# Some 3,900 multiplications of constants ahead of a decoder step's first product

## The chip, the cores and the metric

The kernel runs on one core of one Trainium2 chip. The metric is the device time of one execution in microseconds (us). Before the change it is 1596.22 us, the median of two runs (1596.18 and 1596.26).

## The reference

One inference step of a one-layer decoder for 256 prompt tokens and 8 samples of 4 tokens each, 288 tokens in all, width 2048. Conditioning vectors (one for the prompt, one for each sample, 9 in all) give six modulation vectors; the tokens go through a normalised, modulated projection, a short gated convolution beside a spatial gating mixer, an output product, and a gated feed-forward layer.

```python
mod = (silu(c) @ w_ada + b_ada)                    # 9 x 12288, the conditioning product
h   = rms(x, g_mix) * (1 + sc_m) + sh_m
proj = h @ w_in                                    # 2048 x 9216
b_gate, c_gate, hc, u, v, ga, gb = split(proj)
ya = b_gate * conv(c_gate * hc)                    # width 3
yb = gelu(u) * (causal w_sg @ rms(gelu(v), g_v) + b_sg)
merged = sigmoid(ga) * (ya @ w_pa) + sigmoid(gb) * (yb @ w_pb)
x = x + gt_m * (merged @ w_out)
gate, up = split((rms(x, g_ffn) * (1 + sc_f) + sh_f) @ w_ffn_in)
x = x + gt_f * ((silu(gate) * up) @ w_ffn_out)     # d_ff 5632
y = rms(x, g_final)
```

Beside y, the last rows of the convolution's input and the normalised v rows are returned. All inputs and outputs are fp32.

## The kernel before, in words

All of it is held with features on the partitions and the 288 tokens along the free dimension. A weight tile of 128x128 is the stationary operand, an activation tile of 128x288 the moving one.

**The products.** Weights and activations are split into a high part in fp32r and a low part, the fp32r of what is left. `triple` (L239 to L244) then issues three matmuls: high by high, high by low, low by high. The casts for the high parts run on ScalarE (L471), the subtractions for the low parts on VectorE (L478, L258). These three lines of `triple` are most of the program. Tiles of the moving operand, made by `slot`, begin 7 elements (28 bytes) into a buffer of 320 (`LEADIN`, `PITCH`). In the first stretch they are 298 columns wide, elsewhere 288. For fp32 and fp32r there is no separate weight load in the program; the profile still shows one LDWEIGHTS record for each matmul record.

**The conditioning product** (`Ada.run`, L403) is plain fp32: the 9 vectors, padded to 32 columns, are stationary, and up to 512 columns of `w_ada` move. Four such matmuls with the same accumulator tile `ada` go to four groups of 32 columns of the array (`tile_position=(0, 32 * j)`). A plain fp32 matmul is two records in the profile, so four make eight.

**The beginning.** `warm` (L595) multiplies a bf16 tile of ones by itself, 288 columns wide, into a PSUM tile `idle` that nobody reads. TensorE's program begins with `warm(24)`, the first conditioning block `a0[0]`, `warm(5)`, `a0[1]` with `warm(6)` in its middle, 2 and 6 more of `warm`, and then the first projection stream `w0` with 298 columns. After eight tiles of `w0` comes `a1[0]`, after eleven `a1[1]`.

**What sets the order.** TensorE's order is the order in which the code is written (a manual schedule). VectorE, ScalarE and SyncE are ordered by a scheduler until the head of the program starts, and by hand in the head. All weights are loaded by SyncE's queue (SP) into one pool of 7 buffers of 8 KB per partition, tag `raw`; a load waits until the earlier tile of its buffer has been read for the last time, and all later loads wait behind it on the queue. The head loads both blocks of `a0` (`raw`, 1 MB each), four pieces of `w0` with the first tile of `x` between them, both blocks of `a1`, the second tile of `x`, then `wK`, `wA` and the rest of `x`.

**PSUM.** Tiles tagged `main` turn through four banks; `idle` holds the first.

Of the kernel before, what the change touches and what calls it, by code (L numbers as in the profile page):

```python
# [8 lines left out]
F32 = mybir.dt.float32  # L9
F32R = mybir.dt.float32r  # L10
# [4 lines left out]
P = 128  # L15
D = 2048
T = 288
# [10 lines left out]
RAW = 7  # L28
# [60 lines left out]
def decoder_kernel(tc, d):  # L89
    nc = tc.nc  # L90
    from contextlib import ExitStack

    with ExitStack() as es:
        def pool(name, bufs=1, **kw):
            return es.enter_context(tc.tile_pool(name=name, bufs=bufs, **kw))

        pc = pool("const")
        pw = pool("wstream")
        pslot = pool("slots", MAIN)
        pkept = pool("kept", KEPT)  # L100
        ptmp = pool("tmp", 5)
        pps = pool("psum", 4, space=bass.MemoryType.PSUM)
        with tc.manual_schedule(engines={nc.tensor.engine}):
            _body(tc, nc, d, pc, pw, pslot, pkept, ptmp, pps)


def _body(tc, nc, d, pc, pw, pslot, pkept, ptmp, pps):
    ids = [0]

    def nm(s):  # L110
        ids[0] += 1
        return f"{s}_{ids[0]}"

    def const(name, shape, dt=F32):
        return pc.tile(shape, dt, tag=name, name=name)
# [12 lines left out]
    def psmain():  # L128
        return pps.tile([P, 512], F32, tag="main", name=nm("pm"), bufs=4)
# [4 lines left out]
    V, A, G, PE, SY = nc.vector, nc.scalar, nc.gpsimd, nc.tensor, nc.sync  # L134
# [232 lines left out]
    class Step:  # L367
        defer = False
        raw = None
# [218 lines left out]
    wb = const("wb", [P, 288], BF16)  # L588
    G.memset(wb, 1.0)
    idle = psmain()  # L590
# [498 lines left out]
        tail.close()  # L1089


    rh1 = h1.__getitem__
    def at(main, plan):
        out, n = [], 0
        for s in main:
            out.append(s)
            if isinstance(s, Blk):
                n += 1
                out += plan.pop(n, [])
        assert not plan  # L1100
        return out
# [71 lines left out]
    n = len(steps)  # L1173
# [30 lines left out]
    for s in steps:  # L1204
# [11 lines left out]
        i = pos[id(s)]  # L1216
# [124 lines left out]
```

## Time and profile before

| | |
|---|---|
| median of two runs | 1596.22 us |
| profiled execution | 1596.24 us |
| its span, first to last instruction | 1594.5 us |
| outside the span | 1.74 us |
| TensorE matmul records | 12641 |
| VectorE, ScalarE busy | 1015.9 us, 735.7 us |
| first conditioning matmul starts at | 7.00 us |
| first projection matmul starts at | 12.09 us |

A matmul record's length is modelled and overlaps the next: what one matmul costs is the distance between starts, which the timeline gives to 10 ns, or the count in a stretch that is all matmuls. In the timeline, a row is the start in us, the time covered in us, the engine, the line, the operation, the tiles, stationary shape, moving shape, and how many records the row joins.

### The profile page before, as it was taken

Reading aid. Unit: us, or ns where it says so; the run is one execution under the profiler, and the core shown is the slowest. Engines: PE = TensorE matmul, PEld = TensorE weight load, DVE = VectorE, ACT = ScalarE, POOL = GpSimd, SP = SyncE. Lnnn points to the kernel's source line nnn. Section 1 sums busy time; section 2 is a strip of 40 time slices with the busy share of each in tenths; the row PEclk is TensorE's granted clock in tenths of the full one; section 3 lists DMA queues with packets and bytes.
Section 4 is the critical chain, followed back from the end, with each engine's and each line's share of the span. In section 5 each row is a group of like instructions: output and inputs, shape, how many; then the busy total and the mean of one; then the engine's idle time right before and its main releaser. Section 6 shows DMA issues by size and latency. Waiting matters only on the chain.

```text
span 1594.5 us, 31602 instructions
## 1 busy us (share of the span) xinstructions
PE 1583.4 (99%) x12641; PEld 1518.7 (95%) x12641; DVE 1015.9 (64%) x2200; ACT 735.7 (46%) x1366; POOL 20.9 (1%) x65
## 2 busy tenths in 40 slices
PE   9999999999999999999999999999999999999997
PEld 8998999898998998999898999999999999999997
DVE  6676788877755667667844555555655555555565
ACT  5633344643444434456633444444444444444464
POOL 0000000000000000011000000000000000000000
PEclk9999999999999999999999999999999999999999
DMA  9887866777778766654577556443464534645341
GB/s 382 331 323 285 322 240 218 282 271 313 283 293 333 277 258 228 254 175 170 176 309 268 217 183 217 164 168 118 165 233 163 169 126 164 228 162 174 113 164 60
DMA packets 59476, 357.88 MB, mean 224 GB/s; under 512 B 6720, under 2 KB 10176, under 8 KB 28608
## 3 DMA queue, kind: packets, MB, share of 16 engines
q1 hardware_dynamic: 59040, 355.73, 60.6%
q8 instruction: 99, 1.62, 0.4%
q14 instruction: 49, 0.40, 0.1%
q10 hardware_dynamic: 288, 0.13, 0.0%
HBM read 352.74 MB, written 3.09 MB: 223 GB/s over the span
## 4 chain that ended last, share of the span: by engine, by line
PE 97%; DVE 2%; issue 0%; ACT 0%; DVEq 0%; POOL 0%; ACTq 0%; POOLq 0%
PE pm L239 30%; PE pm L244 30%; PE pm L242 30%; PE ada L403 5%; DVE lo L478 1%; PE pm L595 1%; DVE s L337 0%; DVE st L1070 0%; DVE s L318 0%; DVE t L331 0%; PE px L902 0%; ACT hi L471 0%; PE px L901 0%; PE px L213 0%; PE px L848 0%
## 5 line engine op out<-in xcount | busy, mean ns | idle before, releaser
L239 PE MATMUL pm<-s,hi 128*128 128x288 f32 (+1 forms) x3750 | 1095.4, 292 | 0.3 <-DVE s L998 0.3
L242 PE MATMUL pm<-s,hi 128*128 128x288 f32 (+1 forms) x3750 | 1090.6, 291 | 0.1
L244 PE MATMUL pm<-s,lo 128*128 128x288 f32 (+1 forms) x3738 | 1088.1, 291 | 0.0
L471 ACT CAST hi<-raw 128x512 fp32r<-128x512 f32 (+1 forms) x963 | 585.5, 610 | 774.2 <-PE pm L242 738.2
L478 DVE TENSOR_TENSOR lo<-raw,hi 128x512 fp32r<-128x512 f32 (+1 forms) x849 | 578.6, 683 | 420.0 <-ACT hi L471 407.6
L239 PEld LDWEIGHTS pm<-s,hi 128*128 128x128 f32 x3750 | 702.1, 187 | 15.7 <-issue 13.3
L242 PEld LDWEIGHTS pm<-s,hi 128*128 128x128 f32 x3750 | 702.2, 187 | 0.3 <-DVE s L337 0.3
L244 PEld LDWEIGHTS pm<-s,lo 128*128 128x128 f32 x3738 | 699.9, 187 | 0.0
L258 DVE TENSOR_TENSOR lo<-raw,hi 128x512 fp32r<-128x512 f32 x111 | 74.6, 676 | 28.0 <-ACT hi L471 27.2
L403 PE MATMUL ada<-raw,cs 128*32 128x512 f32 (+2 forms) x1152 | 88.0, 452 | 0.0
L403 PEld LDWEIGHTS ada<-raw,cs 128*32 128x32 f32 x1152 | 30.9, 110 | 44.5 <-issue 41.6
L793 DVE TENSOR_TENSOR s<-pm,s 128x288 f32<-128x288 f32 x72 | 32.8, 456 | 18.5 <-PE pm L244 18.2
L311 ACT CAST s<-t 128x288 fp32r<-128x288 f32 (+1 forms) x76 | 32.9, 433 | 19.1 <-DVE t L825 12.5
L313 DVE TENSOR_TENSOR s<-t,s 128x288 fp32r<-128x288 f32 (+1 forms) x76 | 35.0, 461 | 6.5 <-ACT s L311 5.7
L353 DVE SCALAR_TENSOR_TENSOR x<-pm,mod,x 128x256 f32<-128x256 f32 x79 | 37.5, 475 | 0.0
L991 DVE SCALAR_TENSOR_TENSOR t<-t,pm 128x288 f32<-128x288 f32 x42 | 19.1, 454 | 19.3 <-PE pm L244 19.3
L785 DVE TENSOR_TENSOR s<-pm,s 128x288 f32<-128x288 f32 x48 | 21.8, 454 | 9.9 <-PE pm L244 9.2
L352 DVE TENSOR_TENSOR t<-pm,mod 128x32 f32<-128x32 f32 x79 | 15.1, 192 | 16.5 <-PE pm L244 15.9
L776 DVE TENSOR_TENSOR s<-s,rb 128x288 f32<-128x288 f32 x48 | 21.5, 448 | 0.0
L181 ACT ACTIVATE t<-x 128x288 f32<-128x288 f32 x29 | 12.9, 444 | 17.4 <-DVE x L356 17.4
L186 DVE TENSOR_TENSOR acc<-acc,t 128x288 f32<-128x288 f32 x33 | 15.0, 455 | 8.2 <-ACT t L181 8.2
L770 DVE SCALAR_TENSOR_TENSOR s<-pm,s 128x256 f32<-128x256 f32 x36 | 17.3, 481 | 2.7 <-PE pm L244 2.7
(168 smaller groups left out, 479.5 us busy)
## 6 DMA issues: line engine op xcount, KB each, us to landing
raw<-in_fi SPq DMA_DIRECT2D x84, 1024.0 KB, 4.8
raw<-in_a SPq DMA_DIRECT2D x64, 1024.0 KB, 7.5
raw<-in_f SPq DMA_DIRECT2D x64, 704.0 KB, 4.0
raw<-in_wD SPq DMA_DIRECT2D x34, 1024.0 KB, 5.3
raw<-in_aE SPq DMA_DIRECT2D x16, 1024.0 KB, 9.8
raw<-in_wo SPq DMA_DIRECT2D x16, 1024.0 KB, 5.8
raw<-in_wC SPq DMA_DIRECT2D x19, 768.0 KB, 4.4
raw<-in_pa SPq DMA_DIRECT2D x8, 1024.0 KB, 6.0
```

The lines of the kernel that those rows point to most:

```text
L239: PE.matmul(out, wh, ah, start=first, stop=False)
L242: end_ = PE.matmul(out, wh, al, start=False, stop=turn and last)
L244: end_ = PE.matmul(out, wl, ah, start=False, stop=last)
L258: lows.pop(0)[1]()
L311: A.copy(hi, a)
L313: V.tensor_tensor(lo, a, hi.bitcast(F32), ALU.subtract)
L353: V.scalar_tensor_tensor(x[:, m, :TP], ps[:, :TP], mod[:, gt0 + m, 0:1], x[:, m, :TP], ALU.mult, ALU.add)
L403: PE.matmul(acc[32 * j : 32 * j + 32, :w], cs[:, kt, :], self.raw[:, o : o + w], start=kt == 0, stop=kt == 15, tile_position=(0, 32 * j), ...
L471: A.copy(hi, self.raw[:, s * 128 : e * 128])
L478: sub()
L785: return V.tensor_tensor(part[m], ps[:, :T], part[m], ALU.add)
L793: V.tensor_tensor(a, ps[:, :T], a, ALU.add)
```

## The change

A function `bench` is added and called once, before the first conditioning block is built. It takes four tiles of the `raw` pool: `f`, which VectorE fills with 0.75, and three fp32r copies of it, `r0` by VectorE, `r1` and `r2` by ScalarE. It takes three more banks of the `main` PSUM tiles beside `idle`. Then TensorE multiplies these constants, with `start` and `stop` set on each matmul. Nothing reads the products; nothing that the kernel returns is changed.

```diff
+    def bench():
+        f = pw.tile([P, 2048], F32, tag="raw", name=nm("bench"), bufs=RAW)
+        V.memset(f, 0.75)
+        rs = []
+        for i in range(3):
+            r = pw.tile([P, 2048], F32R, tag="raw", name=nm("benchr"), bufs=RAW)
+            A.copy(r, f) if i else V.tensor_copy(r, f)
+            rs.append(r)
+        r0, r1, r2 = rs
+        outs = [idle] + [psmain() for _ in range(3)]
+        def st(r, i, o=0, m=P):
+            q = o + P * (i % 3)
+            return r[:, q : q + m]
+        def mm(i, s, m, n=512):
+            PE.matmul(outs[i % 4][:, :n], s, m, start=True, stop=True)
+        def group(i, j, s, m, n, w=32):
+            PE.matmul(outs[i % 4][w * j : w * j + w, :n], s, m,
...
+                tile_position=(0, w * j), ...)
+        for i in range(48):
+            PE.matmul(idle[:, :T], wb[:, :P], wb, start=True, stop=True)
+        for n in (512, 510, 508, 496, 480, 448, 384, 320):
+            for o in range(0, 64, 8):
+                for q in range(3):
+                    for i in range(6):
+                        mm(0, st(r0, i), r2[:, o + 512 * q : o + 512 * q + n], n)
+        for o in range(64):
+            for i in range(12):
+                mm(i // 3, st(r0, i), r2[:, o + 512 * (i % 3) : o + 512 * (i % 3) + 512])
+        for o in (0, 7, 16, 23):
+            for b in range(0, 64, 4):
+                for i in range(4):
+                    mm(i, st(r0, i, b), r2[:, o : o + 512])
+                    mm(i, st(r0, i, b), r2[:, o + 512 : o + 1024])
+                    mm(i, st(r1, i, b), r2[:, o : o + 512])
+        for n in (512, 256, 128):
+            for o in (0, 7):
+                for one in (0, 1):
+                    for i in range(8):
+                        for j in range(4):
+                            m = o + 384 * j
+                            group(0 if one else j, j, f[:, 32 * i : 32 * i + 32], f[:, m : m + n], n)
+        for n in (128, 256):
+            for i in range(8):
+                for j in range(4):
+                    m = 7 + 384 * j
+                    group(0, j, f[:, 32 * i : 32 * i + 32], f[:, m : m + n], n)
+                for q in range(6):
+                    mm(1, st(r0, q), r2[:, 7 : 519])
+        for n in (512, 288):
+            for o in (0, 7):
+                for i in range(12):
+                    group(0, 0, st(r0, i, 0, 32), r2[:, o : o + n], n)
...
+        for n in (32, 64):
+            for i in range(48):
+                PE.matmul(idle[:, :n], st(r0, i), r2[:, 7 : 7 + n], start=True, stop=True)
+            for i in range(48):
+                PE.matmul(idle[:, :n], st(r0, 0), r2[:, 7 : 7 + n], start=True, stop=True)
+        for i in range(24):
+            PE.matmul(idle[:, :32], f[:, P * (i % 8) : P * (i % 8) + P], f[:, 7:39], start=True, stop=True)
+        for i in range(24):
+            PE.matmul(idle[:, :P], f[:, P * (i % 8) : P * (i % 8) + P], f[:, 7 : 7 + P], start=True, stop=True)
+
+    bench()
```

The two loops left out are 120 and 96 more 512-wide fp32r matmuls (`mm`, L1110) on `r0`, `r1` and `r2` with moving tiles from columns 7, 519 and 1031.

TensorE's program at its start, before: `wb` is the bf16 tile, `pm_100` is `idle`, `raw_103` the first block of `a0`, `cs` the conditioning vectors. The words in brackets are the counters that a row waits for.

```order
L595 LDWEIGHTS wb [waits Pool_49]
L595 MATMUL pm_100<-wb 128x288
...
L403 MATMUL ada_168<-raw_103,cs 32x64 [waits DMAHW1_49,DVE_49]
L403 MATMUL ada_168<-raw_103,cs 32x64 x15
L403 MATMUL ada_168<-raw_103,cs 32x64 [waits DMAHW3_49]
```

The same place after the change, down to the first conditioning matmul: `benchr_103` is `r0`, `benchr_107` is `r2`, `bench_101` is `f`, `raw_3898` the first block of `a0`.

```order
L1124 LDWEIGHTS wb [waits Pool_49]
L1124 MATMUL pm_100<-wb 128x288
...
L1110 MATMUL pm_100<-benchr_107,benchr_103 128x512 [waits DVE_49,Activation_49]
...
L1110 MATMUL pm_100<-benchr_107,benchr_103 128x320 x144
...
L1171 MATMUL pm_100<-benchr_107,benchr_103 128x64 x48
L1173 MATMUL pm_100<-bench_101 128x32 x24
L1175 MATMUL pm_100<-bench_101 128x128 x24
L595 LDWEIGHTS wb
L595 MATMUL pm_100<-wb 128x288
...
L403 MATMUL ada_3963<-raw_3898,cs 32x64 [waits DMAHW2_49,DVE_49]
```

Every added matmul stands ahead of `warm(24)` and of the first conditioning matmul. The added ones, counted by line and shape over the whole program, are: 48 bf16 at L1124; at L1110 144 each of 510, 508, 496, 480, 448, 384 and 320 columns and 1992 of 512; at L1113 (32 stationary columns) 152 of 512, 160 of 256, 160 of 128 and 24 of 288, of which 24 of 512 and the 24 of 288 are fp32r and the others plain fp32; at L1169 and L1171 96 of 32 and 96 of 64 columns; 24 each at L1173 and L1175.

SyncE's queue before, from the last pieces of `w0` (`raw_109`) to the first load of `wA` (`raw_124`); `raw_115` and `raw_118` are the blocks of `a1`:

```order
L452 DMA raw_109<-in_w 128x512 [waits DMAHW2_49]
L385 DMA raw_115<-in_a 128x1024 [waits DMAHW3_49]
L385 DMA raw_115<-in_a 128x1024 [waits DMAHW4_49]
L385 DMA raw_118<-in_a 128x1024 [waits DMAHW5_49]
L385 DMA raw_118<-in_a 128x1024 [waits DMAHW6_49]
L155 DMA x<-in_x 128x288 [waits DMAHW7_49]
L454 DMA raw_122<-in_wK 128x768 [waits DMAHW0_49]
L454 DMA raw_124<-in_wA 128x1024 [waits DMAHW1_49]
```

The same rows after the change, with `raw_3910` and `raw_3913` for `a1`:

```order
L452 DMA raw_3904<-in_w 128x512 [waits DMAHW2_49]
L385 DMA raw_3910<-in_a 128x1024 [waits DMAHW3_49,PE_49,Activation_49]
L385 DMA raw_3910<-in_a 128x1024 [waits DMAHW4_49]
L385 DMA raw_3913<-in_a 128x1024 [waits DMAHW5_49,DVE_49,PE_49]
L385 DMA raw_3913<-in_a 128x1024 [waits DMAHW6_49]
L155 DMA x<-in_x 128x288 [waits DMAHW7_49]
L454 DMA raw_3917<-in_wK 128x768 [waits DMAHW0_49,Activation_49]
L454 DMA raw_3919<-in_wA 128x1024 [waits DMAHW1_49,PE_49]
```

The order of the loads is the same. The first block of `a1` now goes into the buffer of `f`, which TensorE reads in its last added matmul, so that load and all behind it wait for the end of the added work; both blocks of `a0` and `w0` do not.

More of the change, by code (lines that the diff above doesn't have):

```diff
@@ L1089, in finish @@
         tail.close()
+    def bench():
+        import random
+        f = pw.tile([P, 2048], F32, tag="raw", name=nm("bench"), bufs=RAW)
[13 more added lines that the diff above has]
+        def group(i, j, s, m, n, w=32):
+            PE.matmul(
+                outs[i % 4][w * j : w * j + w, :n],
+                s,
+                m,
+                start=True,
+                stop=True,
+                tile_position=(0, w * j),
+                skip_group_check=True,
+            )
+        for i in range(48):
[32 more added lines that the diff above has]
+                    group(0, 0, st(r0, i, 0, 32), r2[:, o : o + n], n)
+        for i in range(12):
+            for t in range(2):
+                for q in range(2):
+                    for z in range(2):
+                        mm(t, st(r0 if z else r1, t), r2[:, 7 + 512 * q : 7 + 512 * q + 512])
+                mm(t, st(r1, t), r2[:, 7 : 7 + 512])
+        for i in range(12):
+            for t in range(2):
+                for q in range(4):
+                    mm(q, st(r0, i + t), r2[:, 7 + 512 * (q % 3) : 519 + 512 * (q % 3)])
+        for n in (32, 64):
[7 more added lines that the diff above has]
+            PE.matmul(idle[:, :P], f[:, P * (i % 8) : P * (i % 8) + P], f[:, 7 : 7 + P], start=True, stop=True)
```

## The prediction

> **What bounds the kernel now.** I read the page first: span, busy time, then the chain of waits.
>
> ```profile
> span 1594.5 us, 31602 instructions
> PE 1583.4 (99%) x12641; PEld 1518.7 (95%) x12641; DVE 1015.9 (64%) x2200; ACT 735.7 (46%) x1366; POOL 20.9 (1%) x65
> PE 97%; DVE 2%; issue 0%; ACT 0%; DVEq 0%; POOL 0%; ACTq 0%; POOLq 0%
> ```
>
> TensorE is busy all the time and is 97% of the chain. It idles 1594.5 - 1583.4 = 11.1 us in all, at the two ends included. So work put into TensorE's program is paid in full, unless it falls into those 11 us. The question is what one added matmul costs, start to start. The table by stretches gives it for 288 columns (columns: stretch, its length, busy time with the records that start in it, granted clock, DMA share, GB/s):
>
> ```profile
> 7.00:12.00 5.00, 4.94 (x148) 1.00 1.05 410
> 12.00:20.00 8.00, 7.91 (x168) 1.00 1.03 407
> 20.00:50.00 30.00, 29.73 (x242) 1.00 0.95 380
> 1000.00:1200.00 200.00, 200.00 (x1545) 1.00 0.50 170
> ```
>
> From 1000 to 1200 us there is nothing but `triple`: 200.00 / 1545 = 129.4 ns per fp32r matmul of 288 columns with its 128-column weight load. For more columns I need the slope. The timeline has the weight loads of 512-wide plain fp32 conditioning matmuls, which come by fours:
>
> ```profile
> 454.43 0.13 PEld L403 LDWEIGHTS ada<-raw,cs 128*32 128x32 f32 x4 [0.30 <-issue]
> ...
> 456.57 0.13 PEld L403 LDWEIGHTS ada<-raw,cs 128*32 128x32 f32 x4 [0.30 <-issue]
> ```
>
> These are six rows, five steps in 2.14 us: 0.428 us for four records side by side. That is 0.836 ns per column, about twice what fp32r can need at most (129.4 / 288 = 0.449), so I read a record as two passes over its columns: 0.418 ns per column and pass. Two widths of fp32r agree with a slope and no more:
>
> ```profile
> 46.06 0.29 PE L242 MATMUL pm<-s,hi 128*128 128x298 f32 x1
> ...
> 47.39 0.29 PE L244 MATMUL pm<-s,lo 128*128 128x298 f32 x1
> ```
>
> Ten steps in 1.33 us are 133 ns for 298 columns, 3.6 ns (to the 1 ns of rounding) over 288; ten columns at 0.418 are 4.2. So I take T(n) = 129.4 + 0.418 (n - 288) ns. In it 288 x 0.418 = 120.4 is streaming and **9.0 ns a fixed cost**. T(512) = 223.0 ns.
>
> The beginning, where the change lands, is in the timeline:
>
> ```profile
> 1.13 5.94 PE L595 MATMUL pm<-wb 128*128 128x288 bf16 x24 [1.13 <-POOL wb L589]
> 6.66 2.87 SPq L385 DMA_DIRECT2D raw<-in_a  x4
> 7.00 1.12 PE L403 MATMUL ada<-raw,cs 128*32 128x64 f32 x64
> 8.05 0.79 PE L595 MATMUL pm<-wb 128*128 128x288 bf16 x5
> 10.78 1.15 PE L595 MATMUL pm<-wb 128*128 128x288 bf16 x8
> 15.89 1.10 PE L403 MATMUL ada<-raw,cs 128*32 128x64 f32 x64
> ```
>
> The first 24 bf16 matmuls take (7.00 - 1.13) / 24 = 0.245 us each; later ones (1.15 - 0.79) / 3 = 0.12 us. The page's clock reads 1.00 in both, so I take the slow ones as seen: the first 24 of a program.
>
> **The change, part by part.** The counts are those of the built program.
>
> 1. L1110, the sweep of widths: 144 of each of eight widths, which add up to 3658 columns. The sum of T is 8 x 129.4 + 0.418 x (3658 - 8 x 288) = 1601 ns; times 144 it is **230.6 us**.
> 2. L1110, the other 1992 - 144 = 1848 of 512 columns: 1848 x 223.0 = **412.1 us**.
> 3. L1113, fp32r with 32 stationary columns, always on the same group of the array: 24 x (223.0 + 129.4) = **8.5 us**.
> 4. L1113, plain fp32 in sets of four groups. A 512-wide set is two steps of the row above, 0.856 us; 256 wide half of that, 0.428. For 128 the nearest row is a product by the unit matrix:
>
> ```profile
> 453.31 0.29 PE L244 MATMUL pm<-s,lo 128*128 128x288 f32 x1
> 453.54 0.64 PE L866 MATMUL px<-cp,s 128*32 128x128 f32 x16
> 454.00 4.48 PE L403 MATMUL ada<-raw,cs 128*32 128x512 f32 x40
> 458.40 0.40 PE L239 MATMUL pm<-s,hi 128*128 128x288 f32 x1
> ```
>
> Its 16 records, two sets, take 454.00 - 453.54 = 0.46 us, 0.23 a set. So 32 x 0.856 + 40 x 0.428 + 40 x 0.23 = **53.7 us**. Sixteen of these sets alternate with 512-wide fp32r. Entering a set costs 0.23 instead of 0.13 us, and leaving it (458.40 - 454.00) - 10 x 0.428 = 0.12 us: 16 x 0.22 = **3.5 us**.
> 5. L1169 and L1171, fp32r of 32 or 64 columns with 128 stationary columns, 192 of them. Their streaming, 13 or 27 ns, is too short to cover a weight load. The trace has no such fp32r matmul. From above stands the 129.4 of 288 columns; from below the 32-column loads of L866, 0.46 / 16 = 0.029 us. The nearest in kind is the plain fp32 sum with one moving column and 128 stationary ones:
>
> ```profile
> 41.91 0.83 PE L213 MATMUL px<-ones,q 128*128 128x1 f32 x6 [0.20 <-DVE q L611]
> 42.60 0.38 PE L239 MATMUL pm<-s,hi 128*128 128x298 f32 x1
> ```
>
> Six records in 0.69 us are 0.115 us a weight load: 192 x 0.115 = **22.1 us**.
> 6. L1173, plain fp32 of 32 columns: 24, that is 48 records, x 0.115 = **5.5 us**. L1175, 24 of 128 columns, has rows of its own kind:
>
> ```profile
> 543.29 0.38 PE L901 MATMUL px<-s,s 128*128 128x128 f32 x2
> ...
> 543.73 0.39 PE L906 MATMUL px<-s,s 128*128 128x128 f32 x2
> ```
>
> Two steps in 0.44 us: 24 x 0.22 = **5.3 us**.
>
> Parts 1 to 6 add up to **741.3 us**. The 48 bf16 ahead of them take the slow start themselves, 24 x 0.245 + 24 x 0.12 = 8.8 us, and the old 24 behind them then go at 0.12, 2.9 us. So the first conditioning matmul starts at 1.13 + 8.8 + 741.3 + 2.9 = 754.1 instead of 7.00 us: a shift of **747.1 us**.
>
> What else could cost or give something? ScalarE's rows at the beginning:
>
> ```profile
> 4.74 0.32 ACT L164 ACTIVATE t<-t 128x144 f32<-128x144 f32 x1 [1.80 <-DMA t<-in_c]
> 9.20 0.62 ACT L471 CAST hi<-raw 128x512 fp32r<-128x512 f32 x1 [4.13 <-DMA raw<-in_w]
> ```
>
> The constants are made while the bf16 matmuls run: 8.8 us for a fill and three copies of 2048 columns, of which ScalarE's two come last. By its cast rate (the second row: 512 columns in 0.62 us) two copies of 2048 take about 5.0 us, from the 5.1 us at which its activation of the conditioning vectors (the first row) ends. That is 10.1 us, when the bf16 matmuls end at 9.9: a wait near nothing, a microsecond at most.
>
> The added **wait** is on SP's queue: the first block of `a1` waits for the last added matmul, and behind it queue `wK`, `wA` and most of `x`. The 2 MB of `a1` were issued at 6.66 and used at 15.89. Now they go out at the bench's end with nothing under way beside them: 2 MB at 410 GB/s is 5.1 us, and with 2 us to start about 7 us. TensorE reaches them 2.9 us (the old warm-up) plus 15.89 - 7.00 = 8.9 us after that end, 11.8 us. It is covered by 4.7 us. Without that cover each microsecond late would be a microsecond of time, up to some 15 us if the whole head ran at the pace of its loads. On the other side `a0` and `w0` have long landed; but TensorE waited little for them: 0.06 + 0.09 + 0.27 us idle from 7 to 50 us, so the gain is under half a microsecond. The tail is unchanged.
>
> Against the profiled execution's own 1596.24 us (0.02 us over the median of the runs) this gives 1596.24 + 747.1 = **2343 us**.
>
> **The Trainium skill on the term that carries most.** The page "TensorE: Matmul & The Clock Gate", section "Back-to-back issue gap", gives an isolated spacing of N / 2.4 + 2.5 ns, 122.5 ns for 288 columns and 215.8 for 512. The trace agrees for bf16 (0.12 us) and differs for fp32r (129.4), so the measurement decides. By the page, an estimate, the sum would be some 20 us smaller.
>
> **The rivals.**
>
> *A cheaper fixed cost.* All moving fp32r tiles of the kernel start 28 bytes into a buffer and accumulate; the added ones start at many columns and do not accumulate. If the 9.0 ns come from either, they could fall to nothing, as with bf16 (0.12 us against 120.4 ns of streaming): 3048 wide matmuls x 9.0 = 27.4 us less, **2316 us**. For it: bf16 has it so, with the same weight tile size. Against: bf16 differs in type, too. 13%.
>
> *Dearer starts.* Where a weight load and the moving stream get in each other's way, a load of 0.115 us would no longer be hidden. If one wide matmul in eight pays that: 381 x 0.115 = 44 us, **2387 us**; all would be 2694. For it: the trace shows one alignment only. Against: in 200 us the rate is steady for many pairs of buffers. 16%.
>
> *Groups that don't overlap.* Half of the plain fp32 sets write four banks rather than one. If sets ran one after another, 53.7 would be 4 x 53.7, **2504 us**. Against: L403 and L866 both overlap. 3%.
>
> *A price per instruction.* If a 512-wide matmul cost what a 288-wide one does, 129.4 ns, parts 1 to 3 fall by 1152 x 129.4 = 149 against 230.6, and 1872 x 93.6 = 175: **2087 us**. Against: 298 columns cost more than 288. 1%. The same section of that page also gives about 131 ns for a stream of load and matmul pairs at 512 columns; the trace speaks against it, since 288 columns need as much already.
>
> *Not slower.* The work is not done: products that no one reads could be left out of what the chip executes. Then only the `raw` buffers remain, `a1` waiting for the copies until about 10 us instead of 6.66: some 3 us, **1600 us**. It decides from the point where fewer than 32 us of 741 (2%) are executed; TensorE's own idle time, 11.1 us, could never hide the rest. Against: every matmul stands in the built program. 1%.
>
> **How the numbers follow.** The forecast has 66%. Its own range is 2330 to 2355: part 5 between its bounds (-16.5 to +2.8 us), rounding of the slope, a us at either edge. Taking in the cheaper cost below and the dearer starts up to one in eight above, the range is 2312 to 2390, which leaves out half of the dearer case and the three small ones, 13%, and a little for what I haven't listed. 2% is what a measurement tells from no change; 1628 us would be that. Faster 0, within 2% 0.01, slower 0.99.
>
> **What would show it.** L1110 with 3000 records between about 10 and 680 us, 223 ns from start to start at 512 columns at every start column; L1113 with four loads each 0.428 us; L403 first at 754 us; SP silent from the last piece of `w0` until about 751 us; no DMA traffic between; TensorE without idle time there, and the old stages behind it unchanged. A spacing that depends on the start column, or an idle TensorE at the second conditioning block, would make it wrong.

## The result, and the profile after

The changed kernel takes 2390.34 us (two runs, 2388.91 and 2391.77) against 1596.22: a ratio of 1.4975, with a 95% interval of 1.4951 to 1.5000. It was forecast at 2343 us, in a range of 2312 to 2390. The direction and all but 47 us of the 794 us were right; the time lies 0.34 us over the range's upper end. The profiled execution is the longer of the two, 2391.77 us.

The page of the changed kernel: the span and the busy times, the granted clock in 40 slices, and the chain by engine and by line:

```profile
span 2390.0 us, 40171 instructions
PE 2378.7 (100%) x16921; PEld 2164.9 (91%) x16921; DVE 1019.0 (43%) x2202; ACT 739.2 (31%) x1368; POOL 21.9 (1%) x65
PEclk9999999999997899999999999999999999999999
PE 97%; DVE 2%; issue 0%; ACT 0%; DVEq 0%; POOL 0%; ACTq 0%; POOLq 0%
PE pm L1110 28%; PE pm L239 20%; PE pm L244 20%; PE pm L242 20%; PE ada L403 3%; PE pm L1113 3%; PE pm L1171 1%; PE pm L1169 1%; DVE lo L478 1%; PE pm L1173 0%; PE pm L1124 0%; PE pm L595 0%; PE pm L1175 0%; DVE s L337 0%; DVE st L1070 0%
```

TensorE still waits for nobody: its idle time is 2390.0 - 2378.7 = 11.3 us, as it was (11.1). The new thing is the 7 and the 8 in the row of the clock, at a third of the span. The table by stretches shows where (columns: stretch, its length, TensorE's busy time with the records that start in it, granted clock, DMA share, GB/s):

```profile
250.00:600.00 350.00, 350.00 (x1508) 1.00 0.00 1
695.00:744.00 49.00, 49.00 (x217) 1.00 0.07 22
744.50:748.00 3.50, 3.50 (x32) 0.95 0.00 0
752.00:762.00 10.00, 10.00 (x48) 0.50 0.01 2
792.80:799.40 6.60, 6.60 (x49) 0.80 0.00 0
1700.00:1900.00 200.00, 200.00 (x1546) 1.00 0.49 171
```

From 250 to 600 us there are only 512-wide fp32r matmuls: 350 / 1508 = 232.1 ns each, where the sum had 223.0. From 752 to 762 us there are 48 short ones, 10.00 / 48 = 208 ns (213 from start to start) at half the clock, where the sum had 115. The last row is the old work, 200.00 / 1546 = 129.4 ns a matmul, as before.

TensorE's timeline from the short matmuls to the first projection:

```profile
744.54 7.44 PE L1169 MATMUL pm<-benchr,benchr 128*128 128x32 f32 x48
751.83 10.40 PE L1171 MATMUL pm<-benchr,benchr 128*128 128x32 f32 x48
762.07 10.43 PE L1169 MATMUL pm<-benchr,benchr 128*128 128x64 f32 x48
772.31 10.43 PE L1171 MATMUL pm<-benchr,benchr 128*128 128x64 f32 x48
782.55 10.43 PE L1173 MATMUL pm<-bench 128*128 128x32 f32 x48
792.79 6.85 PE L1175 MATMUL pm<-bench 128*128 128x128 f32 x48
799.47 3.10 PE L595 MATMUL pm<-wb 128*128 128x288 bf16 x24
802.50 1.10 PE L403 MATMUL ada<-raw,cs 128*32 128x64 f32 x64
807.92 0.80 PE L525 MATMUL pm<-s,hi 128*128 128x298 f32 x4
```

The short stage takes 799.47 - 744.54 = 54.9 us, and the first conditioning matmul starts at 802.50 us, 48.4 us after the 754.1 of the forecast. From the first projection on, 2390.0 - 807.92 = 1582.1 us are left, 1594.5 - 12.09 = 1582.4 before: everything behind the added work is as it was, to 0.3 us. The beginning of the old work, from its first conditioning matmul to the first projection, takes 5.42 us instead of 5.09.

One row of the change was read wrongly ahead of the result. SyncE's queue:

```profile
722.79 60.78 SPq L385 DMA_DIRECT2D raw<-in_a  x4
784.14 0.38 SPq L454 DMA_DIRECT2D raw<-in_wK  x1
799.67 0.33 SPq L454 DMA_DIRECT2D raw<-in_wA  x1
```

The first block of `a1` does not go into the buffer of `f`, as said in the part on the change, but into that of `r1`, whose last reader ends near 722.5 us; its second block follows the last reader of `r0`, near 782.5, `wK` that of `r2`, and it is `wA` that waits for `f`. The counters in the rows say so: the first load waits for ScalarE, which made `r1`; `f` was made by VectorE. The loads were earlier than thought, and covered either way.

### The profile page after: what moved, and what is told of

It is laid out like the page before. It is cut to its first block, busy times and chain, and to the rows that moved or that the text cites. A ratio compares the mean times of both kernels' runs of the same rounds, so it can differ in the third digit from the quotient of the medians.

```text
span 2390.0 us, 40171 instructions
## 1 busy us (share of the span) xinstructions
PE 2378.7 (100%) x16921; PEld 2164.9 (91%) x16921; DVE 1019.0 (43%) x2202; ACT 739.2 (31%) x1368; POOL 21.9 (1%) x65
## 4 chain that ended last, share of the span: by engine, by line
PE 97%; DVE 2%; issue 0%; ACT 0%; DVEq 0%; POOL 0%; ACTq 0%; POOLq 0%
PE pm L1110 28%; PE pm L239 20%; PE pm L244 20%; PE pm L242 20%; PE ada L403 3%; PE pm L1113 3%; PE pm L1171 1%; PE pm L1169 1%; DVE lo L478 1%; PE pm L1173 0%; PE pm L1124 0%; PE pm L595 0%; PE pm L1175 0%; DVE s L337 0%; DVE st L1070 0%
## 5 line engine op out<-in xcount | busy, mean ns | idle before, releaser
L239 PEld LDWEIGHTS pm<-s,hi 128*128 128x128 f32 x3750 | 702.1, 187 | 15.7 <-issue 13.3
L1110 PE MATMUL pm<-benchr,benchr 128*128 128x512 f32 (+7 forms) x3000 | 671.8, 385 | 0.0
L1110 PEld LDWEIGHTS pm<-benchr,benchr 128*128 128x128 f32 x3000 | 555.5, 188 | 113.8 <-issue 4.9
L417 DVE STREAM_TRANSPOSE ev<-ada 128x512 f32<-128x512 f32 (+2 forms) x9 | 4.8, 536 | 808.7 <-PE ada L403 808.7
L1113 PE MATMUL pm<-bench 128*32 128x256 f32 (+2 forms) x896 | 56.8, 403 | 0.0
L1113 PEld LDWEIGHTS pm<-bench 128*32 128x32 f32 x896 | 25.8, 109 | 30.6 <-issue 24.9
L793 DVE TENSOR_TENSOR s<-pm,s 128x288 f32<-128x288 f32 x72 | 32.8, 456 | 18.5 <-PE pm L244 18.2
L311 ACT CAST s<-t 128x288 fp32r<-128x288 f32 (+1 forms) x76 | 32.9, 433 | 19.3 <-DVE t L825 12.8
```

The lines of the kernel that those rows point to most:

```text
L239: PE.matmul(out, wh, ah, start=first, stop=False)
L311: A.copy(hi, a)
L1110: PE.matmul(outs[i % 4][:, :n], s, m, start=True, stop=True)
L1113: PE.matmul(outs[i % 4][w * j : w * j + w, :n], s, m, start=True, stop=True, tile_position=(0, w * j), skip_group_check=True,)
```

## The experiments

Theory "clock": in a stream of short matmuls the granted clock falls to a half, and this costs 22 us. Its rival, "fixed price": a short fp32r or fp32 record needs 0.213 us by itself, whatever the clock. For the wide ones: the spacing at 512 columns holds something that a fixed 9 ns and 0.418 ns a column do not describe; the candidates are the column rate itself, the weight load, accumulation, the start columns and the data.

**Without the short matmuls.** The six last loops of `bench` are left out, and with them 240 of the added products.

```diff
-        for n in (32, 64):
-            for i in range(48):
-                PE.matmul(idle[:, :n], st(r0, i), r2[:, 7 : 7 + n], start=True, stop=True)
...
-        for i in range(24):
-            PE.matmul(idle[:, :P], f[:, P * (i % 8) : P * (i % 8) + P], f[:, 7 : 7 + P], start=True, stop=True)
```

> Leaves out the six last loops of the added work, the short matmuls of 32, 64 and 128 columns (L1169 to L1175), 54.9 us in the changed kernel's profile from 744.54 to 799.47 us. Theory 'clock' (these short matmuls let the granted clock fall to 0.50, and nothing else does): no stretch at 0.50 is left ahead of the tail, the L1110 groups keep their spacing of about 0.232 us at 512 columns, and the time is 2390 - 55 = 2335 us. Rival 'long load' (the clock falls after some 750 us of dense work, whatever follows): a stretch at 0.50 shows near 750 us all the same, and the time is 2345 us or more. Rival 'fixed price' (each short matmul needs 0.213 us by itself): 2335 us too, so this run doesn't tell it from the first.

Measured: 2335.91 us (2335.67 to 2336.09; ratio to before 1.4634, 1.4612 to 1.4656). The row of the clock has no low slice left:

```profile
PEclk9999999999999999999999999999999999999999
```

So the fall belongs to the short matmuls and not to 750 us of dense work; what each costs by nature is left to the next run.

**The same matmuls in another order.**

```diff
+        while short:
+            for args, kw in short[:8]:
+                PE.matmul(*args, start=True, stop=True)
+            del short[:8]
+            for args, kw in wide[:7] if short else wide:
+                PE.matmul(*args, start=True, stop=True)
+            del wide[:7]
```

> The same matmuls as in the changed kernel, every one, in another order: the 240 short ones are issued in groups of 8, each followed by 7 of the 216 last 512-wide ones. Theory 'clock': between the wide ones the clock stays at 1.00, short ones cost about 0.111 us a record, and the time falls by what the half clock cost, 54.9 - 32.9 = 22 us, to 2368 us. Rival 'fixed price': the short ones still cost 0.213 us each wherever they stand, and the time stays at 2390 us.

Measured: 2368.09 us (2367.79 to 2368.46; ratio 1.4837, 1.4812 to 1.4861), 22.2 us less than the changed kernel for the same work. Two of its stretches, inside the mixed part:

```profile
696.00:760.00 64.00, 64.00 (x392) 1.00 0.05 17
770.00:775.00 5.00, 5.00 (x32) 1.00 0.11 36
```

The clock stays at 1.00, and the time is what 0.115 us a short record had promised. "Fixed price" falls.

**Which streams let the clock fall.** In place of the added work, streams of one width each, with 40 wide matmuls ahead of each. (Of this run and of the three called "One property at a time", "Real weights for the constants" and "Start columns of both operands" there is one execution each; what is read from them is spacing within it, not its time.)

```diff
+        for n in (32, 64, 96, 128, 160, 192, 224, 256):
+            rest()
+            for i in range(96):
+                PE.matmul(idle[:, :n], st(r0, i), r2[:, 7 : 7 + n], start=True, stop=True)
+        for n in (32, 64, 128):
+            rest()
+            for i in range(192):
+                PE.matmul(idle[:, :n], hb[:, P * (i % 3) : P * (i % 3) + P], hb[:, 8 : 8 + n], start=True, stop=True)
```

> In place of the added work: streams of 96 fp32r matmuls of 32, 64, 96, 128, 160, 192, 224 and 256 columns, then 192 bf16 ones of 32, 64 and 128, each stream behind 40 matmuls of 512 columns. Theory 'clock': the streams of 32 and 64 columns begin at 0.111 us and go over to 0.213 us after about 3 us, with the granted clock at 0.50 from there; from 160 columns on the spacing stays at 0.11 to 0.12 us and the clock at 1.00; 96 and 128 are open. Rival 'fixed price' (the weight load isn't overlapped): all widths up to 224 have 0.213 us at a clock of 1.00.

The timeline has the streams of 32, 64, 96 and 128 columns:

```profile
17.47 17.23 PE L1114 MATMUL pm<-benchr,benchr 128*128 128x32 f32 x96
45.37 17.80 PE L1114 MATMUL pm<-benchr,benchr 128*128 128x64 f32 x96
74.87 16.73 PE L1114 MATMUL pm<-benchr,benchr 128*128 128x96 f32 x96
102.76 10.83 PE L1114 MATMUL pm<-benchr,benchr 128*128 128x128 f32 x96
```

The stretches: the first 3 us of 32 columns and what follows, then the later part of 96 columns, 128 and 224 columns, and bf16 of 32 columns:

```profile
17.50:20.50 3.00, 3.00 (x29) 1.00 0.00 0
22.00:34.00 12.00, 12.00 (x58) 0.50 0.00 0
80.00:91.00 11.00, 11.00 (x54) 0.50 0.00 0
103.00:113.00 10.00, 10.00 (x92) 1.00 0.00 0
162.50:172.50 10.00, 10.00 (x92) 1.00 0.01 2
202.50:206.50 4.00, 4.00 (x167) 1.00 0.01 4
```

Up to 96 columns the stream starts at 0.111 us and goes to 0.213 when the clock falls, 3 to 4 us after its start; from 128 columns on the clock stays at 1.00, and the spacing at 0.111 us up to 224 columns and 0.116 at 256. At 0.418 ns a column, TensorE streams for 40 of 111 ns at 96 columns (36%) and for 53 at 128 (48%): the limit for these streams lies between. bf16 of 32 columns, at 0.025 us each, streams 13 of 25 ns, 53%, and keeps the clock. That the share of streaming time is what counts fits all eleven streams; it was not varied by itself. The times between two changes in the trace's records of the clock are whole multiples of 3.413 us: here 10.24, 17.07 and 20.48 us (3, 5 and 6 of them), and in the changed kernel 47.79 us at a half (14). The wide matmuls after a fallen stream start slow, too (40 took 10.8 to 11.9 us, against 9.1 to 9.2 after a stream that kept the clock), so the way back costs some 2 us more.

**One property at a time.** Streams of 96 wide matmuls in place of the added work.

```diff
+        for i in range(96):
+            PE.matmul(idle, hb[:, P * (i % 3) : P * (i % 3) + P], hb[:, 8:520], start=True, stop=True)
+        for o in (7, 4, 5, 6):
+            for i in range(96):
+                PE.matmul(idle, st(r0, i), r2[:, o : o + 512], start=True, stop=True)
+        for n in (256, 288, 320, 384, 448, 480):
+            for i in range(96):
+                PE.matmul(idle[:, :n], st(r0, i), r2[:, 7 : 7 + n], start=True, stop=True)
...
+            PE.matmul(idle[:32, :], st(r0, i, 32), r2[:, 7:519], start=True, stop=True)
...
+            PE.matmul(idle, st(r0, i), r2[:, 7:519], start=i == 0, stop=i == 95)
```

> In place of the added work: streams of 96 wide matmuls, one property changed at a time. Theory 'per column' (the fp32r stream itself needs about 0.45 ns a column, so the 0.1294 us at 288 columns held no fixed 9 ns): at start column 7, 0.1155 us for 256 columns, 0.1295 for 288, 0.1445 for 320, 0.174 for 384, 0.2025 for 448, 0.217 for 480, 0.2305 for 512; bf16 at 512 columns 0.215. Theory of the prediction, 'fixed cost': 0.1294 us + 0.418 ns a column over 288, so 0.223 at 512 columns. Rival 'weight load' (the load of 128 columns takes turns with the stream): with 32 stationary columns 512 wide falls to 0.217 or less. Rival 'accumulation': with start and stop only at the ends of the stream 512 wide falls to 0.223. Start columns 4, 5 and 6 against 7, by the start columns of the changed kernel's trace taken by fours: 2, 6 and 3 ns more at 512 columns, about half of that at 288.

Two stretches of the timeline, 512 columns from start 7 and from start 5:

```profile
30.69 10.14 PE L1111 MATMUL pm<-benchr,benchr 128*128 128x512 f32 x44
75.64 10.08 PE L1111 MATMUL pm<-benchr,benchr 128*128 128x512 f32 x42
```

A record of this shape is 0.39 us long, so the starts lie (10.14 - 0.39) / 43 = 227 ns and (10.08 - 0.39) / 41 = 236 ns apart. Means of all streams, from the starts of their records:

| stream, fp32r unless noted | ns | less the columns at 0.4167 ns |
|---|---|---|
| 256 columns from 7 | 115.6 | 8.9 |
| 288 from 7 | 130.0 | 10.0 |
| 320 from 7 | 144.5 | 11.1 |
| 384 from 7 | 173.3 | 13.3 |
| 448 from 7 | 200.0 | 13.3 |
| 480 from 7 | 213.4 | 13.4 |
| 512 from 7 | 226.7 | 13.4 |
| 512 from 4, 5, 6 | 231.7, 236.0, 233.3 | 18.4, 22.7, 20.0 |
| 288 from 5 | 133.5 | 13.5 |
| 512 from 7, 32 stationary columns | 231.1 | 17.8 |
| 512 from 7, start and stop at the ends alone | 226.7 | 13.4 |
| bf16, 512 from 8 (median) | 216 | 2.7 |

(0.4167 ns is the slope from 384 to 512 columns: (226.7 - 173.3) / 128 = 0.417.) Neither theory holds as it was put. "Per column" had 230.5 at 512 from 7 and "fixed cost" 223.0; the measured 226.7 lies in the middle. Up to 384 columns "per column" holds: 115.6 / 256, 130.0 / 288, 144.5 / 320 and 173.3 / 384 are all 0.451 to 0.452 ns, and nothing is fixed. Above 384 a further column costs 0.417 ns. So what comes on top of 0.4167 ns a column grows in step with the columns, from 8.9 ns at 256 to 13.3 at 384, and then stays. "Weight load" and "accumulation" fall: 32 stationary columns are not cheaper, and accumulating costs the same. The start column matters by 5 to 9 ns at 512 columns, somewhat more than expected.

**Real weights for the constants.**

```diff
-        V.memset(f, 0.75)
+        SY.dma_start(f, d["wA"][0])
...
-        V.memset(hb, 0.75)
+        V.tensor_copy(hb[:, :2048], f)
```

> The run that changed one property at a time, with real weights (a block of w_in) in place of the constant 0.75. Theory: the spacing is that of addresses and columns, not of data: every stream as in that run within 1 ns (226.7, 231.7, 236.0 and 233.3 ns at 512 columns from 7, 4, 5 and 6; 130.0 at 288 from 7), at a clock of 1.00. Rival 'data' (constants are cheap, real data lower the clock or the rate): spacings several per cent longer, or a clock below 1.00.

Measured: 226.7, 231.7, 236.0 and 233.3 ns at 512 columns from 7, 4, 5 and 6, and 130.0 at 288 from 7, at a clock of 1.00. The data make no difference on this one core.

**Start columns of both operands.**

```diff
+        for o in (4, 5, 6, 7):
+            for b in range(64):
+                for i in range(12):
+                    q = b + P * (i % 3)
+                    PE.matmul(idle[:, :T], r0[:, q : q + P], r2[:, o : o + T], start=True, stop=True)
```

> In place of the added work: fp32r matmuls of 288 columns, moving tiles from columns 4, 5, 6 and 7, and for each of these stationary tiles from columns b = 0 to 63 (plus 128 and 256), 12 of each pair. Theory 'moving lines': the moving tile's start modulo 4 columns (16 bytes) sets the cost by itself, so the means over b are 132, 136, 134 and 131 to 132 ns for 4, 5, 6 and 7. Theory 'relative': the distance between the two starts sets it, so for each moving start the cost goes through the same values as b goes through four, and the four means are alike, 133 to 134 ns.

The four stretches, moving start 4, 5, 6 and 7 in this order:

```profile
10.00:110.00 100.00, 100.00 (x759) 1.00 0.07 27
112.00:212.00 100.00, 100.00 (x741) 1.00 0.00 1
215.00:315.00 100.00, 100.00 (x750) 1.00 0.00 1
318.00:416.00 98.00, 98.00 (x753) 1.00 0.00 1
```

131.8, 135.0, 133.3 and 130.1 ns. Taken by b modulo 4, the means at one moving start lie within 0.8 ns (130.3 to 130.8 at start 7). So the moving tile's start counts and the stationary one's does not, and "relative" falls for this part. That it goes by fours, which are 16 bytes, is shown by the last stream of the run that changed one property at a time, with moving starts from 0 to 63: taken by the start modulo 4, its means are 132.4, 135.7, 134.2 and 131.6 ns. Single pairs still differ: at start 7 their means go from 129.3 to some 133.5 ns.

**One start for all wide matmuls.** The run without the short ones, with the moving tiles of the sweep and of the 1536 behind it started at 7, 519 or 1031, and the stationary ones at multiples of 128.

```diff
-                        mm(0, st(r0, i), r2[:, o + 512 * q : o + 512 * q + n], n)
+                        mm(0, st(r0, i), r2[:, 7 + 512 * q : 7 + 512 * q + n], n)
...
-                mm(i // 3, st(r0, i), r2[:, o + 512 * (i % 3) : o + 512 * (i % 3) + 512])
+                mm(i // 3, st(r0, i), r2[:, 7 + 512 * (i % 3) : 7 + 512 * (i % 3) + 512])
...
-                    mm(i, st(r0, i, b), r2[:, o : o + 512])
+                    mm(i, st(r0, i), r2[:, 7 : 7 + 512])
```

> The run without short matmuls, with every moving tile of the width sweep and of the 1536 matmuls behind it started at column 7 (or 512 or 1024 columns on) and every stationary tile at a multiple of 128 columns; counts and widths are the same. Theory 'starts' (the fp32r spacing depends on the start columns, and 7 is a cheap one): by the streams at start 7 of the run that changed one property at a time, 226.7 ns at 512 columns and 225.8, 225, 220, 213.4, 200, 173.3, 144.5 ns at the other widths, the sweep takes 144 x 1.6287 = 234.6 us instead of 239.4 and the 1536 take 348.2 instead of 356.8: 13.4 us less, 2335.9 - 13.4 = 2322.5 us. Rival 'no matter' (the differences by start column come from something else that stays, such as the changing pairs of operands): the time stays at 2336 us. The fixed cost of the prediction would want 230.6 and 342.5 us, 2313 us.

Measured: 2327.22 us (2326.73 to 2327.66; ratio 1.4582, 1.4558 to 1.4607), 8.7 us less than with the many starts. The same stretch of the 512-wide matmuls, first without the short ones, then with one start besides:

```profile
250.00:590.00 340.00, 340.00 (x1466) 1.00 0.00 1
```

```profile
250.00:590.00 340.00, 340.00 (x1485) 1.00 0.00 1
```

231.9 and 229.0 ns. The sweep takes 235.1 us (239.4 before, 234.6 expected), the 1536 take 352.2 (356.8 before, 348.2 expected). So "no matter" falls and "starts" gets two thirds of its 13.4 us. The other third lies in how the tiles are paired: in the 768 that take moving tiles from 7, 519 and 1031 in turn, the distances are 228.4, 230.3 and 230.2 ns, though the three starts are the same modulo 16 bytes. In this run's sweep at 512 columns, where a moving tile stays for six matmuls in one PSUM bank, the first matmul from 519 or 1031 takes 230.6 ns and the last of the six 226.7. So changing the moving tile has a part in it; why stays open.

## Why the prediction was wrong, and what of it was right

**Right.** TensorE bounds the kernel and the added work is paid in full (11.3 us of idle time against 11.1). The set-of-four row for plain fp32 held: the 96 sets ahead of the first alternation take 48.3 us, and by the prediction's prices 48.4, so the groups overlap, in four banks as in one. The wait on SP's queue was covered, with the error about its buffer.

**Right by luck.** L1110 starts at 9.75 us (9.9 forecast), with 24 slow bf16 matmuls ahead of it, as the prediction took "the first 24 of a program" to be slow. They are not a fixed number: in the experiments 12 to 23 of the 48 are slow. The fifth microsecond has 6 records in the changed kernel, and 10 in the run with one stream for each width:

```profile
4.00:5.00 1.00, 1.00 (x6) 1.00 1.03 408
4.00:5.00 1.00, 1.00 (x10) 1.00 1.04 414
```

The slow ones start 0.24 us apart, the later ones 0.122. The trace's first record of the clock, of 1.00, begins within 0.2 us of where they end (at 6.93 us in the changed kernel, 3.97 to 6.73 in the experiments); for the time before it there is no record, and the row shows 1.00 all the same. So the prediction's own rows, 0.245 and 0.12 us, fit a spacing at half the clock and at the full one; it read them as a property of the first 24.

**Wrong: part 5 and part 6, the short matmuls.** The step that failed is the price of 0.115 us a weight load, carried over from rows at full clock. The price itself was right (0.111 us in the first 3 us of the stage, 2368.09 us when the clock is kept). What failed is the unsaid assumption that a TensorE that never idles keeps its clock. 54.9 us were measured and 32.9 forecast: **22.0 us**, and the run in another order takes 22.2 us back. The Trainium skill, page "TensorE: Matmul & The Clock Gate", section "What's actually happening", says that the gate goes by how busy TensorE was in windows of about 3.4 us, and has two states. The runs agree: the records have 1.00 and 0.50 alone, the fall comes 3.0 to 4.2 us after a stream starts, and the changes are multiples of 3.413 us apart. The prediction has no rival in which a stream of short matmuls is at half the clock.

**Wrong: parts 1 and 2, T(n).** The step that failed is the extrapolation from 288 to 512 columns with a fixed cost of 9.0 ns, from two widths ten columns apart and tiles that all start 28 bytes into a buffer. The slope from plain fp32, 0.418 ns a column, is right above 384 columns only. Up to there a column costs 0.451 ns and nothing is fixed: ten columns are 4.2 ns by one and 4.5 by the other, which a reading to 1 ns does not tell apart. The sweep and the 1536 behind it:

```profile
9.75 596.25 PE L1110 MATMUL pm<-benchr,benchr 128*128 128x512 f32 x2688
605.93 48.73 PE L1113 MATMUL pm<-bench 128*32 128x512 f32 x776
```

The sweep took 239.4 us for 230.6, the 1536 356.8 for 342.5: **23.1 us**. Of this, 8.7 us are the start columns (the run with one start). Of the remaining 14.4 us, 9.7 are the spacing at the cheap start (234.6 and 348.2 us for 230.6 and 342.5; 226.7 ns for 223.0 at 512 columns), and the rest is in the pairs. The rival "dearer starts" named the cause of the first share and its sign, but not its size: none of the 1536 lost a whole weight load of 0.115 us (the longest distance is 249 ns), and the start columns cost 8.7 us over 2688 matmuls, 3 ns each on average. "A cheaper fixed cost" had the wrong sign: accumulation makes no difference, and the kernel's own start was the cheapest of the four.

**The small rest**, 3.4 us, is in the alternation of sets with wide matmuls (32.2 us; by the prediction's prices 21.4 for the 96 wide ones, 5.3 for the 16 sets and 3.5 for the changes, 30.2), the last 216 wide ones (49.4 for 48.2) and the 24 + 24 of part 3 (8.7 for 8.5). 22.0 + 23.1 + 3.4 = 48.5 us: by so much, to 0.1 us, the first conditioning matmul came later than forecast.

**The other rivals.** "Groups that don't overlap", "a price per instruction" and "not slower" did not come about. The Trainium skill's isolated spacing for 512 columns (page "TensorE: Matmul & The Clock Gate", section "Back-to-back issue gap"), 215.8 ns, holds for bf16 (216 ns here) and not for fp32r (226.7 at best).

**The range** would have held the time if either miss had come alone. It took in a dearer stream, but the short stage only up to 2.8 us over its term, the row of 288 columns being its end above. The 240 records of 32 and 64 columns in parts 5 and 6 at 0.213 us would have put the bound 23.5 us over their terms. That the upper end came within 0.34 us of the time is luck: it was set by one wide matmul in eight losing a whole weight load, 44 us, which did not happen.

## What to carry to other kernels

A TensorE that never waits can still lose half its clock: when streaming fills well under half of each matmul's time, as with 96 or fewer moving columns behind a 128-column fp32r weight load, put wide matmuls between the short ones; 240 short ones cost 22 us more in one block than in groups of eight. Start moving fp32r tiles at a column that is 3 modulo 4 in its buffer, as this kernel's `LEADIN` of 7 does: against the other three starts that saves 1.7 to 4.7 ns per matmul of 288 columns. And a spacing read at one width and one alignment is a price for that shape alone; a slope from two widths ten columns apart is worth no more than its rounding. Where the same matmul stands in a trace at two spacings, one near twice the other, ask for the clock before calling it a property of the place.

## What the runs showed that was not expected

- The clock falls in a stream without a gap: fp32r of 32, 64 and 96 columns at 0.111 us each go to 0.213 us and 0.50, fp32r of 128 columns stays at 0.111 us and 1.00, bf16 of 32 columns stays at 0.025 us and 1.00.
- The spacing of short fp32r matmuls with 128 stationary columns is 0.111 us at any width from 32 to 224 columns, which points to the weight load; at half the clock it nearly doubles, to 0.213 us (at 32 to 96 columns).
- The clock's changes lie whole multiples of 3.413 us apart: 3, 5, 6 and 14 of them.
- From start 7, an fp32r matmul takes 0.451 ns a column with no fixed cost from 256 to 384 columns, and from there 0.417 ns for each further column up to 512: 13.3 or 13.4 ns over 0.4167 ns a column. Why it does is open; weight width, accumulation and data were tried and are not it.
- It also goes by the moving tile's start modulo 16 bytes: 132.2, 135.2, 133.8 and 130.5 ns at 288 columns for starts 4, 5, 6 and 7, means over 64 stationary starts, and not by the stationary tile's start modulo 16 bytes.
